# Gate/up with half of its k tiles by Strassen, accumulating transfers and a written engine order

## The chip, the core and the metric

The kernel runs on one core of one Trainium2 chip. The metric is device time in microseconds of one execution, as the median over runs. In the trace TensorE appears as PE (its weight loads as PEld), VectorE as DVE, ScalarE as ACT, GpSimd as POOL, and SyncE, which issues most transfers, as SP.

## What is computed

One decoder layer over 256 positions of width 2048: a mixer, a cross attention over 256 memory rows, and a gated MLP, each with a residual, then a final norm. The change touches the MLP; the rest of the reference is left out.

```python
def conv_glu_ffn(h, w_gate, w_up, conv_w, conv_b, w_down):
    gate = causal_dwconv(h @ w_gate, conv_w, conv_b)
    return (jax.nn.silu(gate) * (h @ w_up)) @ w_down
...
        x = x + memory_cross_attention(rms_norm(x, xa_norm_g[l]), mem_h, w_xq[l], w_xkv[l], w_xo[l])
        x = x + conv_glu_ffn(rms_norm(x, ffn_norm_g[l]), w_gate[l], w_up[l], ffn_conv_w[l], ffn_conv_b[l], w_down[l])
    return rms_norm(x, final_norm_g)
```

`w_gate` and `w_up` are 2048 x 5632 (44 tiles of 128 columns), `w_down` is 5632 x 2048; the convolution has 3 taps. All inputs are float32.

## The kernel before, in words

**Precision.** Every float32 operand is split into a rounded high part and the rest. ACT casts to the high part, DVE subtracts it for the low part (`split` for activations, `parts`, L932 to L937, for weights). One product of two operands is high x high, high x low and low x high: three matmuls per 128-row k tile. `product` (L867) does that for two k tiles: 6 matmuls of 128 x 128 by 512 columns.

**Gate/up in blocks.** The 5632 columns are taken in 11 blocks of 512 of gate and 512 of up. The 16 k tiles form four groups `j` of four. In a group the activations are a 2 x 2 block matrix (A11, A12, A21, A22: two halves of the positions by two pairs of k tiles), and the weights are too (B11 gate and B12 up on the first pair, B21 and B22 on the second). A plain group takes 8 products. A Strassen group (in Winograd's form) takes 7, with sums of activations (S3, S5, S6, S7, made once in `stationary`, L731, kept in `hS`) and four sums of weights (t1 = B11+B12, t2 = t1+B22, t3 = B12+B22, and t2+B21), which DVE makes in each block. Before the change group 0 goes by Strassen and groups 1 to 3 plainly (`JS`, `JP`, L950).

**Order in a block (L951 to L1003).** First the Strassen products that need B11, B22, t1, t2, t3; then the combinations `q1`, `u2`, `c22` (L972 to L975); the 24 products of the plain groups; scalings by the norm factor `r3` (L991 to L995); the last two Strassen products; `c11` and `c21`. Six PSUM banks hold `b1`, `b2`, `b3`, `b5`, `b6`, `b7`. The convolution of a finished block (`convolve`: transposes on TensorE, taps on ACT and DVE, silu, product with up, a store to `aspill`) is cut into pieces, and `pump` issues a piece after each product of the next block. Otherwise a list scheduler, with its own estimate of times, places the instructions of each engine.

**Buffers and queues.** SP issues all weight loads (512 KB each) into six `wr` buffers; `parts` has five pairs `wh`, `wl`. Long tiles (32 KB a partition) share three `big` buffers: the weight sums' `ring` (L850 on) takes the place of `oT`, which the output projection xo of the attention reads to its end; `arow` takes the place of `hS`, `aring` that of `hP`, and `fin` that of `ring`. A new tile there waits until all readers of the old one are done.

**Around it.** Before gate/up come the 16 row tiles of xo, each followed by `residual` (L704: two DVE additions, a square on ACT, a sum on POOL) and by `stationary`, which scales the row tile on ACT and, after every fourth, splits four of them into `hP` and makes the S sums into `hS`. After gate/up comes the down stage: 84 steps of 12 matmuls and a last part, with weights through the same `wr`, `wh`, `wl` buffers.

Of the kernel before, what the change touches and what calls it, by code (L numbers as in the profile page):

```python
# [14 lines left out]
AX = mybir.AxisListType  # L15

# [25 lines left out]
def hybrid_trunk(ctx, tc, a, out):  # L42
# [661 lines left out]
    def residual(ps, f, sqa, name):  # L704
        dve.tensor_tensor(xres[:, f, :], ps[:, :T], xres[:, f, :], ALU.add)
        dve.tensor_tensor(xres[:, f, :], ps[:, T:], xres[:, f, :], ALU.add)
        if f == 0:
# [11 lines left out]
    for f in range(16):  # L719
        ps = gemm([unit(a["w_mix"][f], "wm")], lambda k: yT[:, k], [KT], "mix")  # L720
        residual(ps, f, sq2[0], "mix")
        split_scaled(h2T[:, f, 0, :], h2T[:, f, 1, :], xres[:, f, :], pv("xa_g", f))
# [5 lines left out]
    hc = [None]  # L728
    hps = []

    def stationary(f):  # L731
        j = f // 4
        if f == 0:
            hps.append(big("hP", [P, 2, KT, T], F32R))
            hps.append(big("hS", [P, 2, 4, 4, 2 * P], F32R))
        hP, hS = hps
        if f % 4 == 0:
            hc[0] = hq.tile([P, 4, T], F32, name="hc", tag="hc", bufs=2)
        h = hc[0]
        act.activation(h[:, f % 4, :], xres[:, f, :], AF.Copy, scale=pv("ffn_g", f))  # L740
        if f % 4 != 3:
            return
        split(hP[:, 0, 4 * j:4 * j + 4], hP[:, 1, 4 * j:4 * j + 4], h)
# [8 lines left out]
        split(hS[:, 0, j], hS[:, 1, j], fl4)  # L752
# [3 lines left out]
    with tc.tile_pool(name="xa", bufs=1, reuse_waits="tile") as xa:  # L756
# [72 lines left out]
        for f in range(3):  # L829
            u, ps = head[f]  # L830
            gemm_part(ps, lambda k: u(k + 12), osrc, 12, 4, KT)
            residual(ps, f, sq3[0], "xo")
# [3 lines left out]
    for f in range(3, 16):  # L836
        ps = gemm([unit(a["w_xo"][f], "wo")], osrc, [KT], "xo")
        residual(ps, f, sq3[0], "xo")
        stationary(f)
    r3, _, r3run = rnorm(sq3, "r3", False)  # L840
    job("r", r3run)
# [19 lines left out]
    def mixed(w):  # L861
        return lambda j, i: (hS[:, 0, j, w, half(i)], hS[:, 1, j, w, half(i)])
# [27 lines left out]

    def convolve(b, cg, cu):
        if b == head_b:
            ac = acts[b] = fp.tile([P, 4, 2, T], F32R, name="ac", tag="ac", bufs=1)
        else:
            af = acts[b] = fp.tile([P, 4, T], F32, name="af", tag="af", bufs=2)
        for p in range(2):
            yield
            gt, ut = turn("gt"), turn("ut")
            for ps, src in ((gt, cg), (ut, cu)):
                for i in range(2):  # L900
                    for t in range(2):
                        pe.transpose(ps[:, i, half(t)], src[t][:, half(2 * p + i)], cv("ident"))
            yield
            sg = fp.tile([P, 2, T], F32, name="sg", tag="sg", bufs=2)
            for i in range(2):
                f = 4 * b + 2 * p + i
                act.activation(sg[:, i], gt[:, i], AF.Identity, bias=pv("ffn_cb", f), scale=pv("ffn_cw", 3 * f + 2))
                for s in (1, 2):
                    dve.scalar_tensor_tensor(sg[:, i, s:], gt[:, i, :T - s], pv("ffn_cw", 3 * f + 2 - s), sg[:, i, s:],
                                             ALU.mult, ALU.add)  # L910
                yield
            act.activation(sg, sg, AF.Silu)
            yield
            s = slice(2 * p, 2 * p + 2)
            if b == head_b:
                dve.tensor_tensor(sg, ut, sg, ALU.mult)
                yield
                split(ac[:, s, 0], ac[:, s, 1], sg)
            else:
                dve.tensor_tensor(af[:, s], ut, sg, ALU.mult)  # L920
            yield
        if b < head_b:
            nc.sync.dma_start(aspill[b], af)

    raw = lambda b, j, w: fp.tile([P, 2, 512], F32, name="wr", tag="wr", bufs=6)

    def load(b, j, w):
        r = raw(b, j, w)
        nc.sync.dma_start(r, a["w_gu"][b, j, :, w])
        return r  # L930

    def parts(src):  # L932
        h = fp.tile([P, 2, 512], F32R, name="wh", tag="wh", bufs=5)
        l = fp.tile([P, 2, 512], F32R, name="wl", tag="wl", bufs=5)
        act.copy(h, src)  # L935
        dve.tensor_tensor(l, src, h.bitcast(F32), ALU.subtract)  # L936
        return h, l  # L937

    slot = [0]

    def sumtile():
        slot[0] += 1
        return ring[:, slot[0] % 8].rearrange("p (i c) -> p i c", i=2)

    def results():
        return [fp.tile([P, 512], F32, name=n, tag=n, bufs=1) for n in ("c11", "c12", "c21", "c22", "q1", "u2")]

    job("xr", rows_of_x())
    c11, c12, c21, c22, q1, u2 = results()
    JS, JP = (0,), (1, 2, 3)  # L950
    for b in range(NB):  # L951
        b1, b3, b5, b6, b7 = (bank(n) for n in ("b1", "b3", "b5", "b6", "b7"))
        t2s, b21s = {}, {}
        for j in JS:
            f_, l_ = j == JS[0], j == JS[-1]
            b11, b22, b12 = load(b, j, 0), load(b, j, 2), load(b, j, 1)
            product(b1, A11, j, parts(b11), first=f_)
            product(b3, S3, j, parts(b22), first=f_)
            t1, t2, t3 = sumtile(), sumtile(), sumtile()
            dve.tensor_tensor(t1, b11, b12, ALU.add)  # L960
            product(b5, S5, j, parts(t1), first=f_, last=l_)
            dve.tensor_tensor(t2, t1, b22, ALU.add)
            product(b6, S6, j, parts(t2), first=f_, last=l_)
            dve.tensor_tensor(t3, b12, b22, ALU.add)
            product(b7, S7, j, parts(t3), first=f_)
            t2s[j] = t2
            b21s[j] = load(b, j, 3)
        if b == 0:
            drain("r")
        if b:  # L970
            c11, c12, c21, c22, q1, u2 = results()
        act.copy(q1, b1)  # L972
        dve.tensor_tensor(u2, b6, q1, ALU.subtract)
        dve.tensor_tensor(q1, b5, u2, ALU.add)
        dve.tensor_tensor(c22, q1, b7, ALU.subtract)  # L975
        b2 = bank("b2")
        for j in JP:
            f_, l_ = j == JP[0], j == JP[-1]
            w = parts(load(b, j, 1))
            product(b3, A11, j, w)  # L980
            product(b2, A21, j, w, first=f_)
            w = parts(load(b, j, 2))
            product(b3, A12, j, w, last=l_)
            product(b2, A22, j, w, last=l_)
            w = parts(load(b, j, 0))
            product(b1, A11, j, w)
            product(b7, A21, j, w)
            w = parts(load(b, j, 3))
            product(b1, A12, j, w)
            product(b7, A22, j, w)  # L990
        act.activation(c22, c22, AF.Copy, scale=r3[:, 1:2])  # L991
        act.activation(q1, q1, AF.Copy, scale=r3[:, 0:1])
        act.activation(u2, u2, AF.Copy, scale=r3[:, 1:2])
        dve.scalar_tensor_tensor(c12, b3, r3[:, 0:1], q1, ALU.mult, ALU.add)
        dve.scalar_tensor_tensor(c22, b2, r3[:, 1:2], c22, ALU.mult, ALU.add)  # L995
        for j in JS:
            l_ = j == JS[-1]
            product(b1, A12, j, parts(b21s[j]), last=l_)
            dve.tensor_tensor(t2s[j], t2s[j], b21s[j], ALU.add)
            product(b7, A22, j, parts(t2s[j]), last=l_)  # L1000
        act.activation(c11, b1, AF.Copy, scale=r3[:, 0:1])
        dve.scalar_tensor_tensor(c21, b7, r3[:, 1:2], u2, ALU.mult, ALU.subtract)
        job("cv", convolve(b, (c11, c21), (c12, c22)))  # L1003
# [8 lines left out]
    fin = big("fin", [P, 3, D], F32)  # L1012
    for t in range(2):
        nc.sync.dma_start(fin[:, t], xspill[t])
    nc.sync.dma_start(fin[:, 2], a["fin_row"])
# [24 lines left out]
    def rows(k, c):  # L1040
        rw = fp.tile([P, 2, 512], F32, name="wd", tag="wr", bufs=6)
# [5 lines left out]
    for m, (k, c) in enumerate(steps):  # L1047
# [5 lines left out]
        if k % 4 == 2 and c == 0 and 0 < n < NB - 1:  # L1053
            both(n + 1)
        w = rows(k, c)
# [114 lines left out]
```

## Time and profile before

| | us |
|---|---|
| median of 3 runs (1540.8 to 1542.66) | 1542.04 |
| the profiled execution | 1542.11 |
| its span in the trace | 1540.2 |
| TensorE busy | 1500.7 (97%) |
| DVE busy | 1063.2 (69%) |
| ACT busy | 830.3 (54%) |
| POOL busy | 185.5 (12%) |

The span is the time between the first and last instruction in the trace; the execution's own time is a little longer. TensorE's matmuls overlap in its pipeline, so a matmul's printed length is longer than the distance between two starts, and the distance is what counts. In a row of the timeline the bracket at the end tells how long the engine stood idle before the instruction and what released it. PEclk is the granted clock as a share of 2.4 GHz.

### The profile page before, as it was taken

The page shows a single profiled execution, that of the slowest core. Times are in us where ns is not written, and L with a number is a line of the kernel's source. Part 1 is how long each engine was busy: PE and PEld are TensorE (multiplying, and loading weights), DVE is VectorE, ACT ScalarE, POOL GpSimd, SP SyncE. Part 2 cuts the span into 40 slices and gives each one's busy share as a digit, 9 for nine tenths or more (in the row PEclk, how much of TensorE's full clock was granted, in tenths as well). Part 3 has the DMA queues.
Part 4 walks back from the last instruction along what each step waited for, and adds up shares of the span by engine and source line. Part 5 has one row for each costly group of instructions (what it writes and reads, how often), then busy time and mean ns, then how long its engine had stood idle before and what let it go on. Part 6 is the DMA issues. An engine that isn't in the chain of part 4 may idle for free.

```text
span 1540.2 us, 20426 instructions
## 1 busy us (share of the span) xinstructions
PE 1500.7 (97%) x7788; PEld 1273.0 (83%) x7788; DVE 1063.2 (69%) x1407; ACT 830.3 (54%) x1215; POOL 185.5 (12%) x197
## 2 busy tenths in 40 slices
PE   6899999999999999999979999999999999999997
PEld 4788889888888888988868888888888888888886
DVE  6978887676544776666766878887778886555445
ACT  5555665554444554655645666555556665444433
POOL 0432522441000221001220000000000000000000
PEclk9999999999999999999999999999999999999999
DMA  6445443456555555344537666666666678665652
GB/s 234 149 172 187 149 160 124 162 185 239 192 189 189 192 192 190 139 139 162 204 111 251 209 208 194 192 197 211 205 214 203 198 254 306 202 192 192 193 193 80
DMA packets 67090, 290.83 MB, mean 189 GB/s; under 512 B 11312, under 2 KB 11696, under 8 KB 50864
## 3 DMA queue, kind: packets, MB, share of 16 engines
q1 hardware_dynamic: 66848, 289.01, 55.1%
q8 instruction: 61, 1.00, 0.2%
q10 hardware_dynamic: 144, 0.52, 0.1%
q14 instruction: 37, 0.30, 0.1%
HBM read 279.93 MB, written 9.57 MB: 188 GB/s over the span
## 4 chain that ended last, share of the span: by engine, by line
PE 90%; DVE 5%; POOL 1%; ACT 1%; DMA 1%; issue 1%; SPq 0%; DVEq 0%; POOLq 0%; ACTq 0%
PE b L872 10%; PE b L873 10%; PE b L871 10%; PE acc L1037 5%; PE acc L1038 5%; PE acc L1036 5%; PE xq L142 4%; PE xo L142 4%; PE mix L142 4%; PE kk L142 3%; PE pvs L690 2%; PE pvs L689 2%; PE pvs L688 2%; PE xq L143 2%; PE xo L143 2%; PE mix L143 2%
## 5 line engine op out<-in xcount | busy, mean ns | idle before, releaser
L935 ACT CAST wh<-wr 128x1024 fp32r<-128x1024 f32 x165 | 172.4, 1054 | 142.0 <-PE b L873 137.2
L871 PE MATMUL b<-wh,hP 128*128 128x512 f32 x594 | 233.4, 393 | 6.3 <-ACT wh L935 6.3
L936 DVE TENSOR_TENSOR wl<-wr,wh 128x1024 fp32r<-128x1024 f32 x165 | 198.9, 1219 | 51.3 <-ACT wh L935 51.3
L872 PE MATMUL b<-wl,hP 128*128 128x512 f32 x594 | 231.8, 390 | 0.7 <-DVE wl L936 0.7
L873 PE MATMUL b<-wh,hP 128*128 128x512 f32 x594 | 231.9, 390 | 0.0
L936 DVE TENSOR_TENSOR wl<-wd,wh 128x1024 fp32r<-128x1024 f32 x88 | 107.5, 1224 | 103.8 <-ACT wh L935 103.8
L935 ACT CAST wh<-wd 128x1024 fp32r<-128x1024 f32 x88 | 92.5, 1054 | 120.7 <-PE acc L1038 115.7
L871 PEld LDWEIGHTS b<-wh,hP 128*128 128x128 f32 x594 | 111.7, 188 | 29.2 <-ACT wh L935 6.6
L872 PEld LDWEIGHTS b<-wl,hP 128*128 128x128 f32 x594 | 111.8, 188 | 23.9 <-DVE wl L936 1.2
L873 PEld LDWEIGHTS b<-wh,hP 128*128 128x128 f32 x594 | 111.8, 188 | 23.4
L1036 PE MATMUL acc<-wh,aring 128*128 128x512 f32 x320 | 124.5, 389 | 0.0
L1037 PE MATMUL acc<-wl,aring 128*128 128x512 f32 x320 | 124.5, 389 | 0.0
L1038 PE MATMUL acc<-wh,aring 128*128 128x512 f32 x320 | 124.5, 389 | 0.0
L101 DVE TENSOR_TENSOR wil<-wi,wih 128x1024 fp32r<-128x1024 f32 x78 | 100.3, 1292 | 16.7 <-ACT wih L100 16.5
L100 ACT CAST wih<-wi 128x1024 fp32r<-128x1024 f32 x78 | 81.4, 1049 | 19.5 <-PE in_k L142 7.4
L1089 POOL TENSOR_TENSOR fs<-fs,cst 128x1 f32<-128x1 f32 x2 | 1.5, 742 | 728.1 <-DVE fs L1088 728.1
L142 PE MATMUL xq<-h2T,wqh 128*128 128x512 f32 x240 | 84.9, 393 | 0.0
L142 PE MATMUL kk<-mT,wkh 128*128 128x512 f32 x240 | 84.4, 393 | 0.0
L142 PE MATMUL xo<-oT,woh 128*128 128x512 f32 x240 | 84.3, 392 | 0.0
L142 PE MATMUL mix<-yT,wmh 128*128 128x512 f32 x240 | 84.1, 392 | 0.0
L101 DVE TENSOR_TENSOR wvl<-wv,wvh 128x1024 fp32r<-128x1024 f32 x32 | 39.7, 1239 | 45.4 <-ACT wvh L100 45.4
L1036 PEld LDWEIGHTS acc<-wh,aring 128*128 128x128 f32 x320 | 60.1, 188 | 12.6
(464 smaller groups left out, 3622.2 us busy)
## 6 DMA issues: line engine op xcount, KB each, us to landing
wr<-in_w_gu SPq DMA_DIRECT2D x176, 512.0 KB, 5.0
wd<-in_w_down SPq DMA_DIRECT2D x88, 512.0 KB, 4.7
wi<-in_w_in SPq DMA_DIRECT2D x39, 1024.0 KB, 4.9
wk<-in_w_k SPq DMA_DIRECT2D x16, 1024.0 KB, 4.9
wv<-in_w_v SPq DMA_DIRECT2D x16, 1024.0 KB, 4.8
wm<-in_w_mix SPq DMA_DIRECT2D x16, 1024.0 KB, 4.8
wq<-in_w_xq SPq DMA_DIRECT2D x16, 1024.0 KB, 4.9
wo<-in_w_xo SPq DMA_DIRECT2D x16, 1024.0 KB, 4.9
```

The costliest lines, as they stand in the source:

```text
L100: act.copy(hi, src)
L101: return dve.tensor_tensor(lo, src, hi.bitcast(F32), ALU.subtract)
L142: pe.matmul(ps, h, full, start=kk == 0, stop=False)
L143: i = pe.matmul(ps[:, T:], l, xt[:, 0, :], start=False, stop=False)
L871: pe.matmul(ps, xh, wh, start=first and i == 0, stop=False, skip_group_check=True)
L872: pe.matmul(ps, xh, wl, start=False, stop=False, skip_group_check=True)
L873: m = pe.matmul(ps, xl, wh, start=False, stop=last and i == 1, skip_group_check=True)
L935: act.copy(h, src)
L936: dve.tensor_tensor(l, src, h.bitcast(F32), ALU.subtract)
L1036: pe.matmul(acc[t, n], ah, wh, start=first, stop=False)
L1037: pe.matmul(acc[t, n], ah, wl, start=False, stop=False)
L1038: return pe.matmul(acc[t, n], al, wh, start=False, stop=last)
```

## The change

- Groups 0 and 1 go by Strassen, 2 and 3 plainly. `hS` holds two groups.
- A block is a plan of 22 steps, in the order of `KINDS`: a Strassen step is one product, a plain step (`p0` to `p3`) two.
- Each weight is split (`prepare`) four steps before its products, and loaded eight steps before that, into eight `wr` buffers (B11 into `ring`).
- t1 = B11+B12 and t2+B21 are made by a transfer from HBM that POOL issues and that adds into the B11 buffer, so B12 and B21 are read twice. DVE makes the other two sums, at `p1` and `p2`.
- `seq` chains ACT's, DVE's and the transposes' instructions in the order of the text; the convolution's pieces go to fixed steps (`STAGES`) instead of behind products.
- The last xo row tile's residual is placed behind the first two weight splits; its square, scaling and sums (`last_row`) behind the second cast. Row tiles are scaled in groups.
- The results `c11` to `c22` lie in `ring`; the three loads into `fin` move to the second last but one block of the down stage.

```diff
-    hc = [None]
+    JS, JP = (0, 1), (2, 3)
...
+    def scaled_rows(h, f, n):
+        for i in range(n):
+            act.activation(h[:, i, :], xres[:, f + i, :], AF.Copy, scale=pv("ffn_g", f + i))
+        split(hps[0][:, 0, f:f + n], hps[0][:, 1, f:f + n], h)
...
-    r3, _, r3run = rnorm(sq3, "r3", False)
-    job("r", r3run)
...
+    def seq(i):
+        e = i.ins.engine
+        if e in latest:
+            tc.add_manual_dep(i.ins, latest[e], NOSYNC, reason="in the order of the text")
+        latest[e] = i.ins.name
+        return i
...
+    def last_row():
+        squared(15, sq3[0], "xo")
+        scaled_rows(fp.tile([P, 1, T], F32, name="h15", tag="sg", bufs=2), 15, 1)
+        r3, _, run = rnorm(sq3, "r3", False)
+        job("r", run)
+        return r3
...
+    KINDS = ("11", "22", "p1", "s3", "s1", "p2", "s2", "21", "p0", "p3", "s4")
+    USES = {"11": (("b1", A11),), "22": (("b3", S3),), "s3": (("b7", S7),), "s1": (("b5", S5),), "s2": (("b6", S6),),
+            "21": (("b1", A12),), "s4": (("b7", A22),), "p1": (("b3", A11), ("b2", A21)),
+            "p2": (("b3", A12), ("b2", A22)), "p0": (("b1", A11), ("b7", A21)), "p3": (("b1", A12), ("b7", A22))}
...
+        if kind == "11":
+            r = ring[:, 2 * (b % 2) + j].rearrange("p (i c) -> p i c", i=2)
+        else:
+            r = fp.tile([P, 2, 512], F32, name="wr", tag="wr", bufs=8)
...
+    def prepare(b, kind, j):
+        t = raws[b, "11", j] if kind in ("s1", "s2", "s4") else raws[b, kind, j]
+        split_of[b, kind, j] = parts(t, seq)
+        if kind in ("11", "s2"):
+            nc.gpsimd.dma_start(t, a["w_gu"][b, j, :, 1 if kind == "11" else 3], accum_op=ALU.add)
+        if kind == "p1":
+            r = raws[b, "s3", j - 2]
+            seq(dve.tensor_tensor(r, r, raws[b, "22", j - 2], ALU.add))
+        if kind == "p2":
+            r = raws[b, "11", j - 2]
+            seq(dve.tensor_tensor(r, r, raws[b, "22", j - 2], ALU.add))
...
+        if k == 14:
+            seq(dve.tensor_tensor(u2, o("b6"), q1, ALU.subtract))
+            seq(dve.tensor_tensor(q1, o("b5"), u2, ALU.add))
+            seq(dve.tensor_tensor(c22(b), q1, o("b7"), ALU.subtract))
...
+    AHEAD, LOADS = 4, 8
+    STAGES = (4, 6, 7, 8, 10, 12, 13, 15, 17, 18, 19, 21, 24, 25)
...
+    for s in range(LOADS):
+        load(*plan[s])
+    for s in range(-AHEAD, len(plan)):
+        if s + LOADS + AHEAD < len(plan) and s + AHEAD >= 0:
+            load(*plan[s + LOADS + AHEAD])
+        if s == -AHEAD:
+            for q in range(LOADS, LOADS + AHEAD):
+                load(*plan[q])
+        if s + AHEAD < len(plan):
+            prepare(*plan[s + AHEAD])
+        if s == 1 - AHEAD:
+            tc.add_manual_dep(added.ins, less[-1].ins.name, NOSYNC, reason="the last row's sums behind the first parts")
+            with tc.issue_after(cast[-1].ins):
+                r3 = last_row()
...
+        if k == 1 and b:
+            convs[b - 1] = finish_block(b - 1)
+        for c in (b - 1, b - 2):
+            if c in convs and k + NS * (b - 1 - c) in STAGES:
+                next(convs[c])
+        combine(b, k)
+        multiply(*plan[s])
...
-        rw = fp.tile([P, 2, 512], F32, name="wd", tag="wr", bufs=6)
+        rw = fp.tile([P, 2, 512], F32, name="wd", tag="wr", bufs=8)
...
+            if n == NB - 2:
+                fin = big("fin", [P, 3, D], F32)
+                for t in range(2):
+                    nc.sync.dma_start(fin[:, t], xspill[t])
+                nc.sync.dma_start(fin[:, 2], a["fin_row"])
```

## Rows read from the trace of the kernel before

**Rows 1.** The page: busy time by engine, and the chain that ended last.

```profile
PE 1500.7 (97%) x7788; PEld 1273.0 (83%) x7788; DVE 1063.2 (69%) x1407; ACT 830.3 (54%) x1215; POOL 185.5 (12%) x197
...
PE 90%; DVE 5%; POOL 1%; ACT 1%; DMA 1%; issue 1%; SPq 0%; DVEq 0%; POOLq 0%; ACTq 0%
```

**Rows 2.** Windows: eight gate/up blocks, the start of gate/up, the down stage.

```profile
core 0: us, PE busy (x) PEld busy (x) DVE busy (x) ACT busy (x) POOL busy (x), PEclk, DMA share, GB/s
884.40:1236.40 352.00, 352.00 (x1617) 292.45 (x1616) 281.21 (x315) 206.81 (x242) 0.00 (x0) 1.00 0.63 202
796.20:801.30 5.10, 4.40 (x10) 3.12 (x11) 4.84 (x5) 2.00 (x3) 0.00 (x0) 0.50 0.04 12
1290.00:1526.00 236.00, 236.00 (x1050) 195.34 (x1049) 123.55 (x112) 102.56 (x107) 0.00 (x0) 1.00 0.57 184
```

**Rows 3.** TensorE's timeline (start, length, instruction): one run of products, two blocks' transposes.

```profile
845.78 0.39 PE L871 MATMUL b<-wh,hP 128*128 128x512 f32 x1
...
850.99 0.39 PE L873 MATMUL b<-wh,hS 128*128 128x512 f32 x1
851.22 0.60 PE L902 MATMUL gt<-cst,c 128*128 128x128 f32 x4
...
895.23 0.60 PE L902 MATMUL gt<-cst,c 128*128 128x128 f32 x4
```

**Rows 4.** Timeline at the passage from xo to gate/up.

```profile
789.60 0.39 PE L140 MATMUL xo<-oT,woh 128*128 128x512 f32 x1
...
795.15 1.99 ACT L935 CAST wh<-wr 128x1024 fp32r<-128x1024 f32 x2
796.24 0.79 PE L871 MATMUL b<-wh,hP 128*128 128x512 f32 x1 [6.25 <-ACT wh L935]
...
797.69 0.80 PE L872 MATMUL b<-wl,hP 128*128 128x512 f32 x1 [0.66 <-DVE wl L936]
...
803.93 0.50 PE L872 MATMUL b<-wl,hS 128*128 128x512 f32 x1 [0.66 <-DVE wl L936]
...
806.14 0.49 PE L871 MATMUL b<-wh,hS 128*128 128x512 f32 x1 [0.76 <-ACT wh L935]
```

**Rows 5.** DVE's and ACT's groups and DVE's waits in the eight blocks.

```profile
L936 DVE TENSOR_TENSOR wl<-wr,wh 128x1024 fp32r<-128x1024 f32 x120 | 144.8, 1219 | 32.0 <-ACT wh L935 32.0
...
L973 DVE TENSOR_TENSOR u<-b,q 128x512 f32<-128x512 f32 x8 | 5.4, 680 | 0.0
...
L935 ACT CAST wh<-wr 128x1024 fp32r<-128x1024 f32 x120 | 125.7, 1054 | 108.5 <-PE b L873 105.1 <-DVE c L995 1.7 <-DVE ring L964 1.7
...
DVE wl L936 <- ACT wh L935: 43.3, 43, 1.5
```

**Rows 6.** Transfers: issues in the eight blocks, landing of `wr`, a load of `fin`.

```profile
wr<-in_w_gu SPq DMA_DIRECT2D x128, 512.0 KB, 5.0
aspill<-af SPq DMA_DIRECT2D x7, 512.0 KB, 6.5
...
DMA to landing us min/median/max: 3.7/5.0/10.3
...
fin<-in_fin_row SPq DMA_DIRECT2D x1, 1024.0 KB, 10.4
```

**Rows 7.** Timeline: a DVE addition beside one of POOL, and one alone.

```profile
780.48 1.34 POOL L712 TENSOR_TENSOR sq<-sq,xos 128x256 f32<-128x256 f32 x1 [0.79 <-ACT xos L711]
...
781.14 0.97 DVE L748 TENSOR_TENSOR ss<-hc 128x256 f32<-128x256 f32 x1
...
793.74 0.42 DVE L750 TENSOR_TENSOR ss<-hc,ss 128x256 f32<-128x256 f32 x1 [2.83 <-POOL ss L749]
```

**Rows 8.** The tile `hS`: its last matmuls; SP's timeline: the first `arow` loads.

```profile
L873 PE MATMUL b<-wh,hS x88: 389/393/628, 800.8 to 1252.1; 128*128 128x512 f32 x88
...
1252.53 0.80 SPq L1009 DMA_DIRECT2D arow<-aspill  x2
```

More of the change, by code (lines that the diff above doesn't have):

```diff
@@ L915, in convolve @@
             if b == head_b:
-                dve.tensor_tensor(sg, ut, sg, ALU.mult)
+                seq(dve.tensor_tensor(sg, ut, sg, ALU.mult))
                 yield
-                split(ac[:, s, 0], ac[:, s, 1], sg)
-            else:
-                dve.tensor_tensor(af[:, s], ut, sg, ALU.mult)
+                seq(act.copy(ac[:, s, 0], sg))
+                seq(dve.tensor_tensor(ac[:, s, 1], sg, ac[:, s, 0].bitcast(F32), ALU.subtract))
+            else:
+                seq(dve.tensor_tensor(af[:, s], ut, sg, ALU.mult))
+                yield
+                if p == 1 and b < head_b:
+                    nc.sync.dma_start(aspill[b], af)
@@ L933, in parts @@
+    def parts(src, put=lambda i: i):
         h = fp.tile([P, 2, 512], F32R, name="wh", tag="wh", bufs=5)
         l = fp.tile([P, 2, 512], F32R, name="wl", tag="wl", bufs=5)
-        act.copy(h, src)
-        dve.tensor_tensor(l, src, h.bitcast(F32), ALU.subtract)
+        cast[:] = [put(act.copy(h, src))]
+        less[:] = [put(dve.tensor_tensor(l, src, h.bitcast(F32), ALU.subtract))]
         return h, l
[L939 to L943, printed above, removed]
@@ L945, in results @@
-    def results():
-        return [fp.tile([P, 512], F32, name=n, tag=n, bufs=1) for n in ("c11", "c12", "c21", "c22", "q1", "u2")]
-    job("xr", rows_of_x())
[L949 to L968, printed above, removed]
-            drain("r")
[L970 to L1003, printed above, removed]
@@ new lines, in hybrid_trunk @@
+    cast, less = [], []
+    raws, held, split_of, bk = {}, {}, {}, {}
+    ctile = lambda b, n: ring[:, 4 + 2 * (b % 2) + n // 2, (n % 2) * 512:(n % 2 + 1) * 512]
+    c11, c12, c21, c22 = (lambda b, n=n: ctile(b, n) for n in range(4))
+    KINDS = ("11", "22", "p1", "s3", "s1", "p2", "s2", "21", "p0", "p3", "s4")
+    USES = {"11": (("b1", A11),), "22": (("b3", S3),), "s3": (("b7", S7),), "s1": (("b5", S5),), "s2": (("b6", S6),),
+            "21": (("b1", A12),), "s4": (("b7", A22),), "p1": (("b3", A11), ("b2", A21)),
+            "p2": (("b3", A12), ("b2", A22)), "p0": (("b1", A11), ("b7", A21)), "p3": (("b1", A12), ("b7", A22))}
@@ new lines, in multiply, with combine @@
+    def multiply(b, kind, j):
+        w = split_of.pop((b, kind, j))
+        for n, (name, stat) in enumerate(USES[kind]):
+            begins = (b, name) not in bk
+            if begins:
+                bk[b, name] = bank(name)
+            ends = name in LAST.get(kind, ()) and j in (JS[-1], JP[-1])
+            product(bk[b, name], stat, j, w, begins, ends)
+    def combine(b, k):
+        o = lambda name: bk[b, name]
+        if k == 3:
+            held["q1"], held["u2"] = (fp.tile([P, 512], F32, name=n, tag=n, bufs=1) for n in ("q1", "u2"))
+            seq(act.copy(held["q1"], o("b1")))
+        q1, u2 = held.get("q1"), held.get("u2")
+        if k == 14:
+            seq(dve.tensor_tensor(u2, o("b6"), q1, ALU.subtract))
+            seq(dve.tensor_tensor(q1, o("b5"), u2, ALU.add))
+            seq(dve.tensor_tensor(c22(b), q1, o("b7"), ALU.subtract))
+        if k == 16:
+            for t, s in ((c22(b), 1), (q1, 0), (u2, 1)):
+                seq(act.activation(t, t, AF.Copy, scale=r3[:, s:s + 1]))
+        if k == 18:
+            seq(dve.scalar_tensor_tensor(c12(b), o("b3"), r3[:, 0:1], q1, ALU.mult, ALU.add))
+            seq(dve.scalar_tensor_tensor(c22(b), o("b2"), r3[:, 1:2], c22(b), ALU.mult, ALU.add))
+        if k == 21:
+            seq(act.activation(c11(b), o("b1"), AF.Copy, scale=r3[:, 0:1]))
@@ L1004, in hybrid_trunk @@
+    for _ in convs[NB - 2]:
+        pass
+    job("cv", finish_block(NB - 1))
     drain("xr")
```

85 lines of the change are left out of this document (50 added, 35 removed).

## The prediction

> **What bounds the kernel now.** I read the page's engine shares and chain first: TensorE is busy 97% of the span, and 90% of the chain that ended last is TensorE's own work [rows 1]. So time comes off only where TensorE gets fewer instructions, or where it stands still. The windows say which of the two holds where [rows 2]. In eight ordinary gate/up blocks it is busy 352.00 of 352.00 us at full clock, in the down stage 236.00 of 236.00. There no shorter wait on another engine is worth anything. DVE is busy 281.21 of the 352 (35.2 us a block, 80%), ACT 25.9 a block, POOL nothing, the DMA engines 63%.
>
> TensorE's timeline gives the prices [rows 3]. From 845.78 to the transposes at 851.22 it starts 24 matmuls: 5.44 / 24 = 0.2267 us each. The 0.39 us in a row is a matmul's length in the pipeline, not its cost. The same transposes of the next block start at 895.23, so a block takes 44.01 us. It holds 31 products of 6 matmuls: 186 x 0.2267 = 42.17; the other 1.84 are its 16 transposes.
>
> The one place where TensorE stands still in this part is the start of gate/up [rows 4]. The last matmul of xo begins at 789.60, the first of gate/up at 796.24 after 6.25 us idle: last row's sums, its split, the weight's cast, in that order on ACT. Then it waits 0.66 (797.69), 0.66 (803.93) and 0.76 us (806.14) for weight parts, and runs at a granted clock of 0.50, the 1.2 GHz level, from 796.2 to 801.3 [rows 2]. The first block's products begin at 796.24, the second's 12 matmuls before 851.22, at 848.50: 52.3 us. At full speed it would be 42.2 and 3.7 for its 32 transposes of x, 45.9. So this passage costs 6.25 + 6.4 = 12.6 us.
>
> **Products.** A k group by Strassen takes 7 products, a plain one 8. Two plus two groups make 14 + 16 = 30 products, where one plus three made 31. Each block loses 6 matmuls, 1.36 us; 11 blocks, 66 matmuls: 15.0 us, all on the path. A block should take 180 x 0.2267 + 1.84 = 42.64 us.
>
> **DVE and ACT.** The split pairs go from 19 to 22 a block. Three more subtractions at 1.219 are 3.7 us of DVE, three more casts at 1.054 are 3.2 of ACT [rows 5]. The weight sums on DVE stay four: two Strassen groups need eight, and four go to transfers. DVE becomes 35.2 + 3.7 = 38.8 of 42.6 us, 91%; ACT 29.0. Both stay under TensorE, so I cost this at nothing; what hides it is that splits run four steps ahead, three to four times 1.36 us. Without that cover DVE's waits count: it now waits 43.3 us in eight blocks for casts, 5.4 each [rows 5].
>
> **The written order.** The new wait I can place is on b7. The combination at step 14 reads b7 before p0's second product, three products (4.1 us) later, may add to it. DVE reaches the read after a released part buffer, a cast (1.05), a subtraction (1.22) and three 0.68 us combinations [rows 5]: 4.3 us, 4.5 with some delay between the engines. That is 0 to 0.4 us a block, less if the second pair of transposes falls between: 0 to 4.6 in all, and I take 1.0. Behind these reads on DVE stand only the next subtractions, which have their lead. The last block's remaining convolution steps run beside the down stage, as now: nothing.
>
> **Accumulating transfers.** Four a block, issued by POOL, which has no other work there. The trace shows none, so I bound them. A plain 512 KB weight load takes 0.63 x 352 / 135 = 1.64 us of all sixteen engines (128 loads and 7 stores [rows 6]), which is the low end: an addition cannot move less. High end: the store of the same size, which reads SBUF, lands in 6.5 us; taken as if it held every engine so long, 6.5. An accumulating transfer reads HBM and SBUF and writes SBUF, so I take a load plus a store, 3.3. DMA per block is then 27.7 + 4 x 3.3 = 40.9 us of 42.6: hidden, barely (34.3 and 53.7 at the ends). As to lateness: a first sum is issued when 11 is split and read by s1's cast eight steps later, two of them double: 2 x 2.72 + 6 x 1.36 = 13.6 us, less cast and subtraction 2.3, so 11.3; TensorE runs dry some 6 us after that. A load (5.0) and a store (6.5) in a row would be 11.5. I cost it at nothing, with this the thinnest cover of the change.
>
> The row of the plain load would leave the transfers' rival (below) far off: at 1.64 us a transfer is 2.1 us short of the point where it decides. The Trainium skill ("Collectives: The Full Stack", Why ReduceScatter is half of AllGather) says that an adding transfer reads two sources through one queue and so runs at half a copy's rate. By that rule, an estimate from its factor of two, the four would cost 13.1 us a block instead of 6.6, the sum would be 1524 by either, and the point would be 0.4 us away; no row here shows an adding transfer.
>
> POOL's descriptors could meet DVE: beside a POOL addition lasting 1.34 us a two-input DVE addition took 0.97 us, elsewhere 0.42 [rows 7]. If each transfer did that once, 4 x 0.55 = 2.2 us more DVE a block: 41.0 of 42.6, still under.
>
> **The start of gate/up.** The first weights now go into the ring, which takes the place of oT, and xo's last matmul reads oT. The rows of a like case: the arow loads, which take hS's place and fetch blocks stored long before, issue at 1252.53, after the last matmul on hS began at 1252.1 [rows 8]. So the first load leaves SP as xo ends, lands in 3.7 to 5.0 us [rows 6], and the cast takes 1.05: TensorE idles 4.8 to 6.1 us instead of 6.25. SP's queue holds the other first loads; if they stand behind that one they land up to 3 us later. The first wait for a subtraction (0.66) and the slow clock stay. The two later waits (1.4) and the losses beside them shrink, since four steps are split ahead and row 15's sums move behind the first parts (they are needed only at the twelfth step). I take 1.0 + 3.0 = 4.0 us back; ends: 0, and 12.6 if nothing waits.
>
> **Moved loads.** Three 1 MB loads for the end move from before the down stage to about 8 of its steps (22 us) before they are read; the slowest lands in 10.4 us [rows 6]. SP's weight loads behind them have eight buffers of 2.7 us each. Nothing; if the cover failed, some 5 us. Two loads are issued twice in the first block: 3.3 us of DMA, hidden. Fewer scalings and sums for the two plain groups fall beside xo's matmuls: nothing.
>
> **The sum.** The profiled execution took 1542.11 us (span 1540.20), 0.1 above the median of 1542.04. 1542.1 - 15.0 - 4.0 + 1.0 = 1524 us. Its own range: 1514 to 1531.
>
> **Rivals.** *No start gained back* is inside that range. *The passage vanishes*: ring free earlier, 1542.1 - 15.0 - 12.6: about 1514. For: the loads are all asked for ahead; against: rows 8.
>
> *DVE sets the block*: with its in-order cast waits (5.4) kept, 38.8 + 5.4 = 44.2 us a block, 1.6 over TensorE's, x 11 = 17 us: 1541. For: 91% in a fixed order, and the waits of now; against: those waits come while TensorE is never late, so they are slack.
>
> *Accumulating transfers bind* (slower): decisive from 3.7 us of all engines each ((42.6 - 27.7) / 4), or from landing later than 11.3 us. At 5 us each DMA needs 47.7 a block: 5.1 x 11 = 56 us more, 1580; at 6.5 about 1645. For: 41 of 42.6 leaves nothing for bursts, and the price is the one not seen; against: the midpoint fits.
>
> **The numbers.** Forecast 0.60, passage vanishing 0.07, DVE 0.15, transfers 0.18. About 0.2% (3 us) is what a measurement here can tell from no change: DVE's case splits 0.05 faster, 0.06 same, 0.04 slower. Faster 0.72, same 0.06, slower 0.22. The range runs from the vanished passage to just beyond DVE's case, 1514 to 1543, leaving out the transfers; the likeliest case's own is above.
>
> **What would show it.** Right: about 66 fewer matmuls on b; transposes of successive blocks 42.6 us apart; TensorE full in the blocks; DVE near 91%; idle at the start 5 to 6 us, with no waits of 0.7 after 800. Wrong: TensorE waiting for ACT casts released by a DMA from POOL and a DMA share at 1.0 (transfers); TensorE waiting for DVE's subtractions with DVE without gaps, or for the read of b7 (DVE).

## The result and the profile after

The changed kernel takes 1533.78 us (median of 4 runs, 1532.92 to 1536.45) against 1542.35 of the kernel before beside it: a ratio of 0.9948, with a 95% interval of 0.9931 to 0.9965. That is 8.6 us less. The forecast was 18 less.

First the page of the changed kernel: busy time by engine, and the chain that ended last. A mark such as [rows 1] names the same view of the kernel before.

```profile
PE 1490.8 (97%) x7722; PEld 1261.1 (82%) x7722; DVE 1099.3 (72%) x1435; ACT 856.4 (56%) x1247; POOL 221.5 (14%) x237
...
PE 82%; DVE 7%; DMA 4%; ACT 2%; POOL 2%; issue 1%; SPq 1%; POOLq 0%; ACTq 0%; DVEq 0%
```

TensorE has 66 matmuls fewer, as counted. But its own work has fallen from 90% of the chain to 82%, and DVE, DMA and POOL stand in it. Most of that fall says nothing of the change: of the 126 us that TensorE lost on the chain, 80 lie in the first 440 us, ahead of gate/up, where the chain only goes another way. Only 37 lie between 790 and 852. The windows of the changed kernel say more [rows 2]: eight blocks, the last of xo, the first block.

```profile
884.40:1226.40 342.00, 342.00 (x1570) 281.50 (x1569) 309.58 (x339) 226.62 (x266) 27.85 (x32) 1.00 0.87 258
...
765.00:790.00 25.00, 25.00 (x146) 21.98 (x145) 13.85 (x17) 11.57 (x18) 6.28 (x5) 1.00 0.12 43
...
797.00:852.00 55.00, 49.92 (x215) 39.47 (x216) 38.45 (x38) 32.50 (x40) 8.16 (x8) 0.92 1.02 345
```

In eight blocks TensorE is full, DVE 309.58 / 342 = 91%. In the first block TensorE is busy 49.92 of 55 us, and the DMA share is 1.02, against 0.87 later. (A packet counts whole in the window in which it starts, so a share can pass 1.) TensorE's timeline of the changed kernel [rows 3, 4] shows the places:

```profile
791.00 0.39 PE L141 MATMUL xo<-oT,woh 128*128 128x512 f32 x1
796.89 0.79 PE L882 MATMUL b<-wh,hP 128*128 128x512 f32 x1 [5.50 <-ACT wh L960]
798.15 0.79 PE L883 MATMUL b<-wl,hP 128*128 128x512 f32 x1 [0.47 <-DVE wl L961]
...
808.46 0.66 PE L896 MATMUL xtp<-cst,xres 128*128 128x128 f32 x4 [1.66 <-ACT xt L898]
...
835.89 0.50 PE L883 MATMUL b<-wl,hP 128*128 128x512 f32 x1 [0.51 <-DVE wl L961]
...
839.08 0.50 PE L882 MATMUL b<-wh,hP 128*128 128x512 f32 x1 [2.45 <-DVE ring L1019]
...
857.81 0.27 PE L922 MATMUL gt<-cst,ring 128*128 128x128 f32 x1
...
1242.64 0.27 PE L922 MATMUL gt<-cst,ring 128*128 128x128 f32 x1
...
1279.96 0.39 PE L1094 MATMUL acc<-wh,ac 128*128 128x512 f32 x1
```

and, of the kernel before, the down stage's first matmul:

```profile
1288.62 0.39 PE L1036 MATMUL acc<-wh,ac 128*128 128x512 f32 x1
```

From 857.81 to 1242.64 lie nine blocks: 42.76 us each. The transposes stand 24 matmuls (5.44 us) into a block, so the second block's products begin at 852.37. To the down stage's first matmul the account is, in us:

| | before | after | difference |
|---|---|---|---|
| xo's last matmul to the second block | 58.90 (789.60 to 848.50) | 61.37 (791.00 to 852.37) | +2.5 |
| ten further blocks | 440.12 | 427.59 | -12.5 |
| together, to the down stage | 499.02 | 488.96 | -10.1 |

Of these 10.1 us 1.4 are lost ahead of gate/up: xo's last matmul begins 1.4 us later here, as does its first (696.1 and 694.7). In the fourteen profiles of this study the last one begins anywhere from 789.48 to 792.57, so nothing is read from that. **Below, each kernel is also given by the stretch from xo's last matmul to the down stage's first**, 499.02 before and 488.96 after, which this scatter doesn't touch. Each stretch is read from one profile. Two kernels below whose medians agree within 0.02 us differ by 1.5 us in it, so a difference of that size is not read as a cause.

So the blocks did what was forecast, and the first block lost it again. Ahead of that block SP's timeline of the changed kernel shows a pause of 25 us: the two `ring` loads stand first, wait for xo, and all other loads stand behind them.

```profile
756.82 9.54 SPq L110 DMA_DIRECT2D wo<-in_w_xo  x3
791.41 0.80 SPq L987 DMA_DIRECT2D ring<-in_w_gu  x2
792.32 15.97 SPq L987 DMA_DIRECT2D wr<-in_w_gu  x10
```

In the kernel before, the same view has weight loads during xo:

```profile
765.05 35.25 SPq L929 DMA_DIRECT2D wr<-in_w_gu  x7
```

The other new thing is on ACT. Here are its waits between 790 and 850 in the changed kernel (what waited, for what: us in total, times, longest). `xt` holds the transposed rows of x on their way to `xspill`:

```profile
ACT xt L898 <- DMA xspill<-xt: 8.8, 5, 2.7
```

The same view of the kernel before has no wait for a store; there the copies wait for TensorE:

```profile
ACT xt L887 <- PE xtp L885: 3.7, 4, 1.3
```

The transfers of that stretch (times issued, size, us to landing) show why, first the changed kernel:

```profile
xspill<-xt SPq DMA_DIRECT2D x8, 256.0 KB, 6.8
```

then the kernel before:

```profile
xspill<-xt SPq DMA_DIRECT2D x8, 256.0 KB, 4.4
```

`xt` has two buffers, so a copy into it waits for the store of the copy before last. Before, that store was always in time. Now it isn't, and ACT, which works in a fixed order, holds its weight casts behind the copy. The timeline of the changed kernel shows what that leads to on ACT and DVE:

```profile
833.04 0.59 ACT L898 COPY xt<-xtp 128x512 f32<-128x512 f32 x1 [2.27 <-DMA xspill<-xt]
...
833.53 2.94 ACT L960 CAST wh<-wr 128x1024 fp32r<-128x1024 f32 x3
...
834.61 2.36 DVE L961 TENSOR_TENSOR wl<-wr,wh 128x1024 fp32r<-128x1024 f32 x2 [2.58 <-ACT wh L960]
...
836.89 0.68 DVE L1017 TENSOR_TENSOR u<-b,q 128x512 f32<-128x512 f32 x1
837.61 0.69 DVE L1018 TENSOR_TENSOR q<-b,u 128x512 f32<-128x512 f32 x1
838.33 0.69 DVE L1019 TENSOR_TENSOR ring<-q,b 128x512 f32<-128x512 f32 x1
```

The copy waits for a store, three casts come at once behind it, two subtractions behind these, then the read of b7, and TensorE's 2.45 us at 839.08 are the wait for that read. The chain that ended last goes the same way (start, length, what): a weight load that takes 10.97 us to land, then three stores of `xt`, which are 33% of the chain between 790 and 852.

```profile
794.57 10.97 DMA wr<-in_w_gu
...
808.43 8.27 DMA xspill<-xt
...
817.41 4.94 DMA xspill<-xt
...
825.60 7.35 DMA xspill<-xt
```

Such waits, and the half clock after the longer ones, make the passage dearer than before. That was a reading; the runs put it to the test.

### The profile page after: what moved, and what is told of

Read it like the earlier page. It is cut to its first block, busy times and chain, and to the rows that moved or that the text cites. A ratio compares the mean times of both kernels' runs of the same rounds, so it can differ in the third digit from the quotient of the medians.

```text
span 1531.6 us, 20542 instructions
## 1 busy us (share of the span) xinstructions
PE 1490.8 (97%) x7722; PEld 1261.1 (82%) x7722; DVE 1099.3 (72%) x1435; ACT 856.4 (56%) x1247; POOL 221.5 (14%) x237
## 4 chain that ended last, share of the span: by engine, by line
PE 82%; DVE 7%; DMA 4%; ACT 2%; POOL 2%; issue 1%; SPq 1%; POOLq 0%; ACTq 0%; DVEq 0%
PE b L882 9%; PE b L884 9%; PE b L883 9%; PE acc L1096 5%; PE acc L1095 5%; PE acc L1094 5%; PE xq L143 4%; PE xo L143 4%; PE mix L143 4%; PE kk L143 3%; PE pvs L691 2%; PE pvs L690 2%; PE pvs L689 2%; PE xq L144 2%; PE xo L144 2%; PE mix L144 2%
## 5 line engine op out<-in xcount | busy, mean ns | idle before, releaser
L960 ACT CAST wh<-wr 128x1024 fp32r<-128x1024 f32 x154 | 160.2, 1050 | 82.4 <-DVE wr L996 30.0
L961 DVE TENSOR_TENSOR wl<-wr,wh 128x1024 fp32r<-128x1024 f32 x154 | 185.2, 1219 | 27.1 <-ACT wh L960 26.0
L882 PE MATMUL b<-wh,hP 128*128 128x512 f32 x484 | 192.4, 398 | 8.0 <-ACT wh L960 5.5
L884 PE MATMUL b<-wh,hP 128*128 128x512 f32 x484 | 191.8, 397 | 0.0
L883 PE MATMUL b<-wl,hP 128*128 128x512 f32 x484 | 190.6, 394 | 1.0 <-DVE wl L961 1.0
L961 DVE TENSOR_TENSOR wl<-ring,wh 128x1024 fp32r<-128x1024 f32 x88 | 106.5, 1220 | 31.9 <-ACT wh L960 31.8
L960 ACT CAST wh<-ring 128x1024 fp32r<-128x1024 f32 x88 | 91.5, 1051 | 63.5 <-PE b L884 24.8
L882 PEld LDWEIGHTS b<-wh,hP 128*128 128x128 f32 x484 | 91.9, 190 | 28.0 <-ACT wh L960 5.8
L883 PEld LDWEIGHTS b<-wl,hP 128*128 128x128 f32 x484 | 91.9, 190 | 20.3 <-DVE wl L961 1.9
L884 PEld LDWEIGHTS b<-wh,hP 128*128 128x128 f32 x484 | 91.8, 190 | 18.8
L993 POOL DMA_DIRECT2D ring<-in_w_gu x44 | 38.5, 879 | 422.2 <-DVE sg L932 343.1
```

Source lines behind the costliest of these rows:

```text
L882: pe.matmul(ps, xh, wh, start=first and i == 0, stop=False, skip_group_check=True)
L883: pe.matmul(ps, xh, wl, start=False, stop=False, skip_group_check=True)
L884: m = pe.matmul(ps, xl, wh, start=False, stop=last and i == 1, skip_group_check=True)
L960: cast[:] = [put(act.copy(h, src))]
L961: less[:] = [put(dve.tensor_tensor(l, src, h.bitcast(F32), ALU.subtract))]
```

## The experiments

Times are medians; ratios are to the kernel before, which ran beside each, with 95% intervals. Where a kernel was run once, there is no interval, and its time is one reading.

### The six `wr` loads ahead of the `ring` loads

```diff
-    for s in range(LOADS):
+    for s in (*range(2, LOADS), 0, 1):
         load(*plan[s])
```

> The six first wr loads (B22, p1, s3) are issued ahead of the two first ring loads; nothing else is changed. Theory A (the fill is late): in the changed kernel SP issued nothing from 766 to 791.4 because a ring load, which waits for xo's last matmul, stood at the head of its in-order queue, so all first loads fell into the first block, where the DMA engines then run at a share of 1.0. Six loads of 1.64 us of all engines, 9.8 us, move into xo: the first block falls from 55.6 to about 48 us, the whole from 1533.8 to about 1527 (1524 to 1530), and the idle before the first product stays near 5.5, since the first ring load cannot come earlier. Theory B (the accumulating transfers alone overload the first block): it stays within 2 us of 1533.8. Theory C (the order on DVE, with the read of b7 in the first block late by itself): no change, and the 2.45 us wait of TensorE at b for c22 is still there.

1534.78 us, 0.9948 [0.9933, 0.9963]; the stretch is 489.41, the changed kernel's 488.96. The loads did leave earlier, by SP's timeline:

```profile
772.77 3.14 SPq L987 DMA_DIRECT2D wr<-in_w_gu  x6
790.75 0.80 SPq L987 DMA_DIRECT2D ring<-in_w_gu  x2
```

but nothing came of it. Theory A falls in this form. ACT's waits in the same window told what to look at next: the copies of `xt` now wait longer for their stores, and the last one begins at 833.00, where it began at 833.04.

```profile
ACT xt L898 <- DMA xspill<-xt: 10.3, 4, 5.6
```

### The first block's B11 in `wr` buffers

```diff
-        if kind == "11":
+        if kind == "11" and b:
             r = ring[:, 2 * (b % 2) + j].rearrange("p (i c) -> p i c", i=2)
```

> The first block's two B11 tiles lie in wr buffers instead of ring, so that no load of the first block waits for xo's last matmul. Theory A: all eight first loads are issued during xo, the first product follows xo's last matmul at once: the 5.5 us idle goes to under 1, the first block falls from 55.6 to 46 to 48 us, 10 to 14 us less: 1520 to 1524. Theory B: only the idle goes, 1528, and the first block still loses some 8 us to late casts. Theory C: the same 1528, with the wait at b7 kept. A price that all theories allow: six wr buffers instead of eight are left to the other loads of the first block, which could cost 1 to 3 us.

1532.75 us, 0.9928 [0.9910, 0.9946]; stretch 488.45. The idle of 5.5 us is gone: the first product begins at 789.99, 0.24 after xo's last matmul. TensorE gave nearly all of it back in eight later waits, 9.3 us together, and ACT's waits, in the same view, grew to nearly twice those of the changed kernel:

```profile
ACT xt L898 <- DMA xspill<-xt: 15.8, 4, 6.7
```

The first block has a floor that isn't TensorE's: starting it 6 us earlier only lengthens the waits.

### p2 loaded once

The two loads at steps -2 and -1, which repeat those at step -4, are left out.

```diff
-        if s + LOADS + AHEAD < len(plan) and s + AHEAD >= 0:
+        if s + LOADS + AHEAD < len(plan) and s >= 0:
```

> The two p2 loads of the first block are issued once instead of twice; nothing else is changed. The first block is DMA bound by theories A and B: 1 MB less at the some 360 GB/s of that stretch is 2.9 us less: 1531 (1530 to 1532.5). Theory C, or if the second copies land where DMA has room: no change, 1533.8 within 1.

1532.54 us, 0.9936 [0.9919, 0.9953]; stretch 486.44, 2.5 less than the changed kernel, near the 2.9 expected. The median is only 1.2 us less, inside the scatter of the runs, so that bytes in the first block cost time is likely by this run, not shown.

### No accumulating transfers in the first block

```diff
-        if kind in ("11", "s2"):
+        if kind in ("11", "s2") and b:
```

> The four accumulating transfers of the first block alone are left out, so that in that block s1, s2 and s4 use unfinished sums. They take 2.9 us of all engines each by the share of their queue, 11.7 us in all. Theory A: the first block is bound by DMA, whatever is taken out of it: 5 to 9 us less, 1525 to 1529, about the same as from moving the fill. Theory B: 8 to 11 less, more than the moved fill brings. Theory C: no change.

1529.33 us, 0.9906 [0.9886, 0.9927], 4.5 us under the changed kernel; stretch 482.68, 6.3 less. The stores land in 4.7 us instead of 6.8, and of the copies' waits, in the view of ACT's waits, one is left:

```profile
ACT xt L898 <- DMA xspill<-xt: 1.9, 1, 1.9
```

Theory C falls: the read of b7 is late only because the casts are, and TensorE had no wait for it here. The size fits A's 5 to 9 better than B's 8 to 11, but A had fallen with the first run. What fits all four, and the chain of the changed kernel, is a chain through the stores, theory D.

### `xt` in eight places of its own

```diff
-            xt = fp.tile([P, 512], F32, name="xt", tag="sg", bufs=2)
+            xt = ctile(q // 4, q % 4)
```

> The transposed rows of x (xt, eight copies on ACT, each then stored to xspill) get eight places of their own in ring, the later result tiles, instead of two buffers; nothing else is changed. Theory D (formed after the moved fill brought nothing): in the first block each copy of xt waits for the store of the copy before last, and as ACT works in a fixed order the weight casts stand behind it. In the changed kernel these waits are 2.15, 1.26, 0.37, 2.71 and 2.27 us, 8.8 in all, and the casts of p0 and p3 behind them make TensorE wait 0.51 and 2.45 us and then run 1.6 us at half clock. By D these go, and with them 4 to 7 us: 1527 to 1530, and no cast waits for an xspill store. Theory E (the bytes of the first block, wherever they queue): the same bytes flow, so no more than 1.5 us are gained, and the copies' waits turn into waits of casts for loads.

1527.62 us, 0.9904 [0.9887, 0.9920]; stretch 483.40, 5.6 less than the changed kernel. In the view of ACT's waits no copy waits for a store any more, though the stores have become slower, by the view of the transfers from 790 to 852:

```profile
xspill<-ring SPq DMA_DIRECT2D x8, 256.0 KB, 9.0
```

The DMA share is 1.04 from 796 to 846, and TensorE's waits at 835.89 and 839.08 have gone. That is D, and it speaks against E: the same bytes are just as tight, but no copy waits for a store. The bytes are not free, though: TensorE still waits 1.14 us at 806.74, and the chain goes from there back to a weight load that took 10.52 us to land.

### The three edits together

`xt` in `ring`, the first B11 in `wr`, p2 loaded once.

```diff
+            xt = ctile(q // 4, q % 4)
...
+        if kind == "11" and b:
...
+        if s + LOADS + AHEAD < len(plan) and s >= 0:
```

> Three edits together: xt in ring, the first block's B11 in wr buffers, p2 loaded once in the first block. Theory D: with the casts free of the stores, the start 5.5 us earlier is kept instead of being waited out behind the stores: 1519 to 1523, TensorE idle under 2 us between xo and gate/up. Theory E: about as the B11 in wr buffers alone, 1530 to 1532, with TensorE waiting for casts that wait for loads.

1519.51 us (1518.89 to 1520.17), 0.9847 [0.9832, 0.9862]; stretch 475.04. It is the fastest version, 23.7 us under the kernel before in that comparison and 13.9 of the stretch under the changed one. TensorE's timeline of this kernel goes from xo into gate/up without a gap, and the only waits left in the first block are these two:

```profile
790.21 0.39 PE L141 MATMUL xo<-oT,woh 128*128 128x512 f32 x1
790.44 0.40 PE L882 MATMUL b<-wh,hP 128*128 128x512 f32 x1
...
794.66 0.60 PE L166 MATMUL r3ps<-cst,sq 128*128 128x1 f32 x4 [1.32 <-POOL sq L716]
...
799.14 0.66 PE L896 MATMUL xtp<-cst,xres 128*128 128x128 f32 x4 [0.61 <-ACT ring L898]
```

The early B11 was worth 0.5 us of the stretch alone. On top of `xt` in `ring` it and p2 loaded once are together worth 8.4 (483.40 to 475.04; the medians say 8.1). One loss hid the other. How the 8.4 divide between the two edits wasn't tried; the next run, which has p2 loaded once but not the early B11, is only 1.0 under `xt` in `ring` alone, so most of it is likely the early B11.

### The six loads ahead, with `xt` in `ring` and p2 loaded once

```diff
+            xt = ctile(q // 4, q % 4)
...
+    for s in (*range(2, LOADS), 0, 1):
...
+        if s + LOADS + AHEAD < len(plan) and s >= 0:
```

> xt in ring, the six first wr loads issued ahead of the ring loads, p2 loaded once. The idle of 5.5 us before the first product stays, as the first ring load waits for xo. Theory D: 1526 to 1528, 1 to 3 us under xt in ring alone, since the first sums no longer wait for loads. Theory E: 1530 to 1532.

1527.84 us, 0.9901 [0.9886, 0.9915], D's range; the stretch, 482.41, is 1.0 under that of `xt` in `ring` alone, the median isn't under it. Issuing the other loads early brings nearly nothing as long as the first cast waits for `ring`.

### The norm's column sums behind the fifth product

The version of three edits, with the job that sums the squares on TensorE started at step 4.

```diff
         r3, _, run = rnorm(sq3, "r3", False)
-        job("r", run)
-        return r3
+        return r3, run
...
+        if s == 4:
+            job("r", r3run)
```

> The three edits of the run before (xt in ring, first B11 in wr buffers, p2 loaded once), and the norm factor's column sums on TensorE moved from behind the first product to behind the fifth. In the run before TensorE stood 1.32 us at them, waiting for POOL's last sum, and 0.61 us at the second transposes of x. If these are real losses on the path they go: from xo's last matmul to the first block's transposes 51 to 52 us instead of 53.1, in all 1517 to 1518.5. If the wait only moves (the copies of x, behind the same ACT work): 1519.5 as before.

1519.49 us, 0.9860 [0.9845, 0.9875]; stretch 476.51. No gain: from xo's last matmul to the first block's transposes it is 54.3 us (789.48 to 843.80), not 51 to 52. In TensorE's timeline the two waits have become one:

```profile
801.18 1.10 PE L896 MATMUL xtp<-cst,xres 128*128 128x128 f32 x4 [1.83 <-ACT ring L898]
```

They were 1.32 and 0.61 us, together hardly more than the 1.83.

### Every accumulating transfer twice

```diff
-            nc.gpsimd.dma_start(t, a["w_gu"][b, j, :, 1 if kind == "11" else 3], accum_op=ALU.add)
+            for _ in range(2):
+                nc.gpsimd.dma_start(t, a["w_gu"][b, j, :, 1 if kind == "11" else 3], accum_op=ALU.add)
```

> Every accumulating transfer is issued twice, eight a block instead of four, so the sums made by them are wrong by one summand. This prices one in the steady blocks. DMA is busy 0.85 of 42.7 us there, 36.3; at 2.9 us of all engines each, the share of their queue, four more make 47.9 a block, DMA bound: 5 us a block more, some 57 in all, 1590. At a plain load's 1.64 us it would be 42.9 a block, 1534 to 1537. If their lateness and not their bytes decides, with two in a row landing after some 15 us against the 11.3 they have, TensorE waits for s1's casts: 3 to 4 us a block, 1570 to 1580, with the DMA share under 1.

1710.69 us (one run): 177 more than the changed kernel, 16 a block. First the queue of POOL's transfers on the page of this kernel (packets, MB, share of 16 engines):

```profile
q0 software_dynamic: 12672, 46.14, 14.7%
```

ACT's waits in two blocks, 1000 to 1118:

```profile
ACT wh L960 <- DMA ring<-in_w_gu: 46.0, 7, 11.7
```

And POOL's timeline there:

```profile
1005.60 0.86 POOL L994 DMA_DIRECT2D ring<-in_w_gu  x1 [14.57 <-DVE sg L932]
1007.65 0.86 POOL L994 DMA_DIRECT2D ring<-in_w_gu  x1 [1.18 <-DVE wl L961]
1013.75 0.88 POOL L994 DMA_DIRECT2D ring<-in_w_gu  x1 [5.24 <-DMA ring<-in_w_gu]
```

The price holds: 0.147 x 1708.9 / 88 = 2.85 us of all engines each. The DMA share of that window is 0.83, under the 0.87 of the changed kernel's blocks, so the bytes alone don't set the block. The second addition into a tile is issued only when the first has landed (1005.60 to 1013.75 is such a pair), so a sum takes two landings of 8.3 us (their median in that window), over the 11.3 us it has. Lateness decides, as the third expectation had it, but at four to five times its size: 23 us of cast waits a block, 16 us of time.

### Plain loads in place of the accumulating ones

```diff
-            nc.gpsimd.dma_start(t, a["w_gu"][b, j, :, 1 if kind == "11" else 3], accum_op=ALU.add)
+            nc.gpsimd.dma_start(t, a["w_gu"][b, j, :, 1 if kind == "11" else 3])
```

> On the changed kernel, the four transfers a block that add into their tile become plain loads of the same source into the same tile, from the same queue; the sums then are the second summand alone. It prices the adding: by the queue's share an adding transfer takes 2.9 us of all engines and lands in 7.4 us; a plain one should take 1.5 to 1.7 and land in 4.5 to 5.5. The steady block stays at 42.7, as its DMA was not binding; the first block, where it was, gains 2 to 4 us: 1530 to 1532. If the adding costs nothing of its own, the share and the landing stay as they are.

1528.27 us (one run); stretch 484.11, blocks still 42.76 (852.80 - 5.44 to 1274.97, ten blocks). The stretch is 4.9 less than the changed kernel's, somewhat more than expected. Here are the rows of this kernel's page, and then those of the changed kernel:

```profile
q0 software_dynamic: 6336, 23.07, 4.4%
...
ring<-in_w_gu POOLq DMA_DIRECT2D x44, 512.0 KB, 5.8
```

```profile
q0 software_dynamic: 6336, 23.07, 8.4%
...
ring<-in_w_gu POOLq DMA_DIRECT2D x44, 512.0 KB, 7.4
```

Of all engines a plain one takes 0.044 x 1526.5 / 44 = 1.53 us, an adding one 0.084 x 1531.6 / 44 = 2.92. Packets and bytes are the same; the adding costs 1.9 times. It adds 1.6 us to the landing.

### DVE's weight sums twice

```diff
-            seq(dve.tensor_tensor(r, r, raws[b, "22", j - 2], ALU.add))
+            for _ in range(2):
+                seq(dve.tensor_tensor(r, r, raws[b, "22", j - 2], ALU.add))
```

> On the changed kernel, each of DVE's weight sums at p1 and p2 is made twice, four additions a block more; the sums then hold the second summand twice. It asks how far DVE is from setting the block. DVE is busy 38.2 to 38.6 of 42.7 us; four more at 1.14 us from start to start make 42.9. Theory: DVE's waits are slack, so the block stays at 42.7 to 43.5, up to 8 us in all. Rival (the forecast's DVE case): the waits in its fixed order do not shrink, 5 us of them stay, and the block becomes 46 to 48, 40 to 55 us in all.

1555.32 us (one run). Ten blocks take 1301.42 - (855.77 - 5.44) = 451.09, so 45.1 each, 2.35 more. One block's window:

```profile
910.33:955.43 45.10, 43.33 (x198) 35.28 (x197) 43.33 (x47) 27.74 (x34) 3.48 (x4) 1.00 0.83 245
```

DVE's waits over 884.4 to 1226.4, 342 / 45.1 = 7.6 blocks:

```profile
DVE wl L961 <- ACT wh L960: 11.2, 16, 0.8
```

The same of the changed kernel, eight blocks [rows 5]:

```profile
DVE wl L961 <- ACT wh L960: 29.9, 32, 2.3
```

Neither number fits; the truth lies between. DVE is busy 43.33 us of 45.1. In the 7.6 blocks TensorE waits 12.8 us, all of it for casts and subtractions, and ACT's longest waits, 42.3 and 39.0 us in all, are for DVE's sums. So DVE sets the block, and of its waits for casts 1.5 us a block remain (11.2 / 7.6), where the changed kernel has 3.7 (29.9 / 8). Most of the waits were slack, but not all: the room that DVE had was about 2.5 us a block (42.76 - 38.7 - 1.5), not 4.

### Without the written order

```diff
     def seq(i):
         e = i.ins.engine
-        if e in latest:
-            tc.add_manual_dep(i.ins, latest[e], NOSYNC, reason="in the order of the text")
         latest[e] = i.ins.name
         return i
```

> The changed kernel without the chains that fix the order of the engines' instructions; the scheduler places them by its own estimate. Theory: in the steady blocks TensorE is full with or without them, so the transposes of successive blocks stay 42.7 to 43 us apart and the whole within 4 us of 1533.8; only the first block may move. Rival: the order is what holds the read of b7 and the convolution in place; without it TensorE waits for one of them, 1 to 3 us a block, 1545 to 1565.

1533.42 us, 0.9947 [0.9931, 0.9964]; stretch 489.54 against 488.96. In sum the written order is worth nothing that can be measured here. The blocks alone are a little shorter without it, 42.61 us each (859.47 to 1242.96, nine blocks) against 42.76.

## Why the prediction was wrong, step by step

**Products: right.** Forecast 66 matmuls and 15.0 us, with 1.0 us back at b7: 42.73 a block. Measured 42.76. Over the ten undisturbed blocks that is 12.5 of the 12.7 us forecast. That the 42.73 fits so closely is luck: TensorE waits for nothing in these blocks, so the wait at b7 didn't come there. The 0.12 us over the 42.64 without it is something else; it goes with the written order (42.61 without), and no run says what in it. In the first block the read of b7 did hold TensorE, 2.45 us, but behind late casts.

**DVE and ACT: right, more narrowly than costed.** 91% forecast and found; DVE's 38.7 us a block (309.58 / 8) leave no room for the 2.2 us that POOL's descriptors might have cost it. TensorE waits for nothing in eight blocks. The doubled sums show how close it was.

**Accumulating transfers: right in the steady blocks.** I took 3.3 us of all engines; they take 2.92. They land in 7.4 us of the 11.3 they have. But this cover was as thin as the forecast said. Of the 32 in the eight blocks the slowest took all of it (min, median, max), and three of ACT's casts waited for them, 3.2 us in all:

```profile
DMA to landing us min/median/max: 5.6/7.3/11.3
```

No matmul waited. The rival, decisive from 3.7 us or 11.3 us, didn't come, and the doubled ones show its second condition at work. The rule of the Trainium skill ("Collectives: The Full Stack", Why ReduceScatter is half of AllGather), stated there of the adding step of a collective, that it runs at half a copy's rate, agrees with the 1.53 and 2.92 measured here. The reason it gives, two reads through one queue, is not tested by any run.

**The start of gate/up: the step that failed.** It said "I take 1.0 + 3.0 = 4.0 us back; ends: 0, and 12.6 if nothing waits". The passage, 12.6 us before, became 61.37 less the last xo matmul's 0.39 and the 44.5 that a first block takes at full speed (42.64 - 1.84 + 3.7): 16.5. So it didn't give 4.0 back, it took 3.9, a miss of 7.9 us, and the end at 0 was no bound.

The first load did leave as xo ended, and the idle was 5.50 us within the 4.8 to 6.1 given. What failed was "the losses beside them shrink". I had costed every transfer against the average of a steady block, and the first block isn't one. Four kinds of transfer meet in it, of which the text had three, as at most 3 us late, hidden, or nothing: the fill of all buffers, held back behind the `ring` loads; the doubled p2 loads, "3.3 us of DMA, hidden", 2.5 when left out (by one profile); four accumulating transfers, 6.3 when left out; and the stores of x, which no step named. In the kernel before the DMA share from 797 to 852 was 0.69, now it is 1.02, and stores that landed in 4.4 us took 6.8. Two buffers of `xt` made ACT wait for them, and ACT's order made the casts wait for ACT. Places of its own for `xt` alone gave 5.6 back. These are not terms of a sum: 2.5, 6.3 and 5.6 are more than the 7.9 missed, because each edit shortens the same waits.

That was not told by any wait in the trace of before: there the copies waited for TensorE alone. What could have been read there is the condition, a transfer in a cycle with two buffers on an engine that also casts weights, at 4.4 us, and the price, once the block's bytes were summed. The stores there are issued at 816.73, 819.33, 822.54, 825.72 and 828.93, so a tile of `xt` comes round after 5.8 to 6.4 us: a landing of 4.4 us fits, one of 6.8 doesn't.

**The vanishing passage.** This rival, 1514, was to come from "ring free earlier". An early first load alone brought 0.5 us. The fastest version, with the stores and p2 changed too, whose first block's transposes start at 843.34, has a passage of 843.34 - 5.44 - 790.21 - 44.9 = 2.8 us of the 12.6 (44.9 is the 44.5 and 0.39 above), and takes 1519.5.

**Moved loads at the end: nothing, as forecast.** From the down stage's first matmul to the span's end it is 1540.2 - 1288.62 = 251.6 before and 1531.6 - 1279.96 = 251.6 after.

## What to carry to other kernels

Sum the transfers of the first block of a loop by itself: the prefetch of all later steps, the last stores of the stage before and each new transfer fall together there, and what an average over steady blocks hides is not hidden in it. For every transfer in a cycle of few buffers ask what engine would wait if it landed half as late again, and what else stands in that engine's order. When one remedy brings nothing, look for a second limit behind it before dropping it: early first loads were worth 0.5 us alone, and together with p2 loaded once 8.4 when the stores no longer held ACT.

## What the runs showed that was not expected

An accumulating transfer of 512 KB takes 1.9 times the engine time of a plain one of the same bytes and packets (2.92 and 1.53 us) but lands only 1.6 us later (7.4 and 5.8), and POOL is busy 879 ns issuing it. In the kernel with doubled additions the second into a tile was issued only after the first had landed, so a sum of three terms made that way takes two full landings.

The price of a wait of TensorE is not only the wait. In the changed kernel its matmuls run 0.43 us apart, with a granted clock of 0.50 (the 1.2 GHz level), from the 5.50 us idle to 802.6, and again from 840.4 to 843.8, behind waits of 0.51 and 2.45 us; behind the wait of 1.66 us at 808.46 it stays at 1.00. The second stretch, eight matmuls at 0.43 instead of 0.23, costs some 1.6 us. In the fastest version no wait in the first block is over 1.32 us, and the granted clock of 790 to 838 is 1.00.

```profile
790.00:838.00 48.00, 46.07 (x221) 37.67 (x220) 37.43 (x38) 31.71 (x40) 8.12 (x8) 1.00 0.99 320
```
